# Nine-row partition pitch for the first two load groups of an RMSNorm-and-repeat kernel

## The chip, the cores and the metric

The kernel runs on one core of a Trainium2 chip. The metric is the device time of one execution in microseconds (us), lower is better. A comparison gives a median over several executions; a profile is one execution, recorded with times of every instruction and every DMA packet.

## The reference

The input `x` is 8 x 512 x 2048 in float32, that is 4096 rows of 2048 numbers (8 KB a row, 33.55 MB in all); `gamma` has 2048 numbers. Each row is repeated twice, divided by its root mean square and multiplied by gamma. The output has 8192 rows, 67.11 MB.

```python
x_rep = np.repeat(x, 2, axis=1)
rms = np.sqrt((x_rep ** 2).mean(axis=-1, keepdims=True) + 1e-6)
return (x_rep / rms * gamma[None, None, :]).astype(np.float32)
```

## The kernel before

The 4096 rows are handled in four groups of 1024 rows, n = 0 to 3. In a group each of the 128 SBUF partitions holds eight neighbouring rows of HBM: `load(n, at)` (L49) moves them with one DMA, 64 KB for a partition and 8.39 MB in all. A group is written in two halves, h = 0 and 1, of four rows a partition: `store(n, h, to)` (L52) writes the four rows twice over, again 64 KB a partition and 8.39 MB. So the program has four loads and eight stores of x's data, twelve DMAs of one size, and all of them are issued by SyncE's queue (SP) in the order of the code.

One SBUF tile `y` of 24 rows a partition is all the room there is. Its three regions of eight rows are called `first` (0 to 7), `second` (8 to 15) and `third` (16 to 23). The order of the work is written out by hand in `four(n, constants, step)` (L89), which does two groups and is called twice, with n = 0 and n = 2:

- Group n is loaded into rows 4 to 11, group n + 1 into `third`. The constants are made between the two issues.
- `squares` (L57) sums the squares of a row on ScalarE (ACT, L63) and takes the root (L67). `scale` (L70) takes the reciprocal on VectorE (DVE, L73) and multiplies a row by it and by gamma (L75), into every second row of a region. `repeat` (L80) copies each finished row to its neighbour (L82), on ACT or on DVE.
- The first half of group n goes to `first` and is stored from there, the second half to `second`. Then the first half of group n + 1 goes to `first`, the second to `third`.

Since all regions are reused, a load waits for the stores that still read its rows: the load of group 2 (rows 4 to 11) waits until the first half of group 1 has left `first`, the load of group 3 until the second half of group 1 has left `third`.

In the second region's repeat, `step` says whether DVE copies its two rows with one instruction (n = 0) or with two (n = 2).

`constants()` (L121) issues gamma's DMAs from ACT's queue: one of 16 pieces of 500 B, and three of 64 B each, into partition 0 of the rows 0 to 2 of `y`. Two GpSimd (POOL) partition broadcasts, L132 and L136, spread them from there to all partitions of `gamma_b`.

Of the kernel before, what the change touches and what calls it, by code (L numbers as in the profile page):

```python
# [1 line left out]

# [4 lines left out]


@with_exitstack
def kernel(  # L10
    ctx: ExitStack,
    tc: tile.TileContext,
    x: bass.AP,
    gamma: bass.AP,
    out: bass.AP,
):
    nc = tc.nc
    P = nc.NUM_PARTITIONS
    f32 = mybir.dt.float32
    Act = mybir.ActivationFunctionType  # L20
    Alu = mybir.AluOpType

    B, S, D = x.shape
    Bo, So, Do = out.shape
    R = So // S
    assert R == 2 and D == Do and B == Bo and So == S * R
    eps = 1e-6
    inv_d = 1.0 / float(D)


    K = 4
    N = B * S
    ntiles = N // (P * K)
    assert N % (P * K) == 0 and ntiles == 8
    H = 2
    x_t = x.rearrange("b s d -> (b s) d").rearrange("(n p k) d -> n p k d", p=P, k=H * K)
    out_t = out.rearrange("b s d -> (b s) d").rearrange("(n p h j) d -> n h p (j d)", p=P, h=H, j=K * R)

    singles = ctx.enter_context(tc.tile_pool(name="singles", bufs=1))
    rows = ctx.enter_context(tc.tile_pool(name="rows", bufs=1))  # L40
    junk = ctx.enter_context(tc.tile_pool(name="junk", bufs=1, space=bass.MemoryType.PSUM))
    small = ctx.enter_context(tc.tile_pool(name="small", bufs=4))

    y = rows.tile([P, 3 * K * R, D], f32, name="y")
    first, second, third = 0, K * R, 2 * K * R

    def load(n, at):  # L49
        nc.sync.dma_start(out=y[:, at : at + H * K, :], in_=x_t[n])  # L50

    def store(n, h, to):  # L52
        nc.sync.dma_start(
            out=out_t[n, h], in_=y[:, to : to + K * R, :].rearrange("p j d -> p (j d)")
        )

    def squares(at, rows):  # L57

        n = len(rows)
        ss = small.tile([P, n], f32, name=f"ss{n}")  # L60
        for c, k in enumerate(rows):
            sq = junk.tile([P, D], f32, name="sq")
            nc.scalar.activation(  # L63
                out=sq[:], in_=y[:, at + k, :], func=Act.Square, accum_out=ss[:, c : c + 1]
            )
        rms = small.tile([P, n], f32, name=f"rms{n}")
        nc.scalar.activation(out=rms[:], in_=ss[:], func=Act.Sqrt, scale=inv_d, bias=eps_t[:])  # L67
        return rms

    def scale(at, to, rows, rms):  # L70
        n = len(rows)
        rstd = small.tile([P, n], f32, name=f"rstd{n}")
        nc.vector.reciprocal(out=rstd[:], in_=rms[:])  # L73
        for c, k in enumerate(rows):
            nc.vector.scalar_tensor_tensor(  # L75
                out=y[:, to + R * k, :], in0=y[:, at + k, :], scalar=rstd[:, c : c + 1],
                in1=gamma_b[:], op0=Alu.mult, op1=Alu.mult,
            )

    def repeat(to, k0, k1, copy):  # L80
        y_r = y[:, to + R * k0 : to + R * k1, :].rearrange("p (k r) d -> p k r d", r=R)
        copy(out=y_r[:, :, 1, :], in_=y_r[:, :, 0, :])  # L82

    ctx.enter_context(tc.manual_schedule())

    half = K // 2
    up, down = list(range(K)), list(range(K - 1, -1, -1))

    def four(n, constants, step):  # L89


        load(n, first + K)
        constants()
        load(n + 1, third)
        for rows in (up[:half], up[half:]):
            scale(first + K, first, rows, squares(first + K, rows))
        repeat(first, 0, half, nc.scalar.copy)
        repeat(first, half, K, nc.vector.tensor_copy)
        store(n, 0, first)
        scale(second, second, down, squares(second, down))  # L100
        repeat(second, half, K, nc.scalar.copy)
        for k in range(0, half, step):
            repeat(second, k, k + step, nc.vector.tensor_copy)
        store(n, 1, second)
        roots = [squares(third + h * K, up) for h in range(H)]
        scale(third, first, up, roots[0])
        repeat(first, 0, half, nc.scalar.copy)
        repeat(first, half, K, nc.scalar.copy)
        store(n + 1, 0, first)
        scale(third + K, third, up, roots[1])  # L110
        repeat(third, 0, K, nc.scalar.copy)
        store(n + 1, 1, third)

    gamma_b = singles.tile([P, D], f32, name="gamma_b")
    G, E = 16, 3
    C = D // G - E
    gamma_s = y[0:1, 0:2, :].rearrange("p k (c d) -> p (k c) d", c=G // 2)
    gamma_t = y[0:1, 2, :]
    eps_t = singles.tile([P, 1], f32, name="eps_t")

    def constants():  # L121
        nc.scalar.dma_start(
            out=gamma_s[0:1, :, :C],
            in_=gamma[: G * C].rearrange("(p c d) -> p c d", p=1, c=G),
        )
        for c in range(E):
            at = G * C + c * G
            nc.scalar.dma_start(
                out=gamma_t[0:1, c * G : (c + 1) * G],
                in_=gamma[at : at + G].partition_broadcast(1),  # L130
            )
        nc.gpsimd.partition_broadcast(  # L132
            out_ap=gamma_b[:, : G * C].rearrange("p (c d) -> p c d", c=G),
            in_ap=gamma_s[0:1, :, :C],
        )
        nc.gpsimd.partition_broadcast(out_ap=gamma_b[:, G * C :], in_ap=gamma_t[0:1, : E * G])  # L136
        nc.vector.memset(eps_t, eps)  # L137

        root = singles.tile([P, 1], f32, name="root")[:]
        nc.scalar.activation(out=root, in_=eps_t[:], func=Act.Sqrt)  # L140

    four(0, constants, half)
    four(2, lambda: None, 1)


# [1 line left out]
_INS = ['x', 'gamma']  # L147
_OUTS = [((8, 1024, 2048), 'float32')]


# [23 lines left out]
```

## Time and profile before

| | us |
|---|---|
| median of 3 executions | 238.38 (238.24 to 238.87) |
| profiled execution | 238.07 |
| its span, first to last instruction or transfer | 236.2 |
| ACT busy | 110.2 (47%) |
| DVE busy | 84.5 (36%) |
| GpSimd busy | 2.8 (1%) |
| share of the 16 DMA engines' span taken by SP's packets (q1) | 98.7% |

The span lies 1.87 us under the profiled execution's own time, which in turn lies 0.31 us under the median. The table says how long each engine had something to do. Neither compute engine is at work for even half of the time; the DMA engines nearly always are.

### The profile page before, as it was taken

The page shows a single profiled execution, that of the slowest core. Times are in us where ns is not written, and L with a number is a line of the kernel's source. Part 1 is how long each engine was busy: PE and PEld are TensorE (multiplying, and loading weights), DVE is VectorE, ACT ScalarE, POOL GpSimd, SP SyncE. Part 2 cuts the span into 40 slices and gives each one's busy share as a digit, 9 for nine tenths or more (in the row PEclk, how much of TensorE's full clock was granted, in tenths as well). Part 3 has the DMA queues.
Part 4 walks back from the last instruction along what each step waited for, and adds up shares of the span by engine and source line. Part 5 has one row for each costly group of instructions (what it writes and reads, how often), then busy time and mean ns, then how long its engine had stood idle before and what let it go on. Part 6 is the DMA issues. An engine that isn't in the chain of part 4 may idle for free.

```text
span 236.2 us, 226 instructions
## 1 busy us (share of the span) xinstructions
DVE 84.5 (36%) x48; ACT 110.2 (47%) x86; POOL 2.8 (1%) x6
## 2 busy tenths in 40 slices
DVE  0000396594699500000000007928919992000000
ACT  2001989479998470000000049991999957400000
POOL 0110000000000000000000000000000000000000
DMA  9898989989898989989898998989898998989894
GB/s 355 356 533 355 510 377 422 466 366 522 355 533 356 533 355 422 466 377 510 355 533 355 488 400 355 533 355 533 355 533 355 488 399 355 533 355 533 355 533 178
DMA packets 1767, 100.68 MB, mean 426 GB/s; under 512 B 230, under 2 KB 230, under 8 KB 230
## 3 DMA queue, kind: packets, MB, share of 16 engines
q1 hardware_dynamic: 1728, 100.66, 98.7%
q10 hardware_dynamic: 38, 0.01, 0.0%
q14 instruction: 1, 0.01, 0.0%
HBM read 33.56 MB, written 67.11 MB: 426 GB/s over the span
## 4 chain that ended last, share of the span: by engine, by line
DMA 45%; ACT 26%; DVE 12%; issue 2%; DVEq 0%
DMA y<-in_x_dram 26%; DMA out_dram<-y 20%; ACT sq L63 15%; DVE y L75 12%; ACT y L82 11%; ACT rms L67 1%; DVE rstd L73 0%; DVEq L75 0%
## 5 line engine op out<-in xcount | busy, mean ns | idle before, releaser
L63 ACT ACTIVATE sq<-y 128x2048 f32<-128x2048 f32 x32 | 60.1, 1878 | 71.1 <-DMA y<-in_x_dram 70.4
L75 DVE SCALAR_TENSOR_TENSOR y<-y,rstd,gamma_b 128x2048 f32<-128x2048 f32 x32 | 73.8, 2349 | 1.6 <-DMA out_dram<-y 1.0
L82 ACT COPY y<-y 128x4096 f32<-128x4096 f32 (+1 forms) x10 | 42.6, 4283 | 19.1 <-DVE y L75 18.3
L73 DVE RECIPROCAL rstd<-rms 128x4 f32<-128x4 f32 (+1 forms) x10 | 1.7, 170 | 109.2 <-ACT rms L67 109.2
L82 DVE COPY y<-y 128x4096 f32<-128x4096 f32 (+1 forms) x5 | 9.2, 1865 | 0.1
L63 ACT ACTIVATION_READ_ACCUMULATOR sq<-y 128x1 f32 x32 | 6.0, 186 | 0.0
L67 ACT ACTIVATE rms<-ss,eps_t 128x4 f32<-128x4 f32 (+1 forms) x10 | 3.0, 297 | 0.3
L140 ACT ACT_TABLE_LOAD x1 | 1.3, 1283 | 2.6 <-issue 2.6
L132 POOL PARTITION_BROADCAST gamma_b<-y x1 | 2.2, 2243 | 10.2 <-DMA y<-in_gamma_dram 10.2
L136 POOL PARTITION_BROADCAST gamma_b<-y x1 | 0.3, 323 | 10.1 <-DMA y<-in_gamma_dram 10.1
L137 DVE MEMSET eps_t<- 128x1 f32 x1 | 0.1, 59 | 0.8 <-PEq L158 0.8
L140 ACT ACTIVATE root<-eps_t 128x1 f32<-128x1 f32 x1 | 0.2, 203 | 0.0
L158 POOL MEMSET const-bfloat16-1.0<- 128x1 bf16 x1 | 0.1, 102 | 0.0
L158 POOL MEMSET const-float32-0.0<- 128x1 f32 x1 | 0.1, 99 | 0.2 <-issue 0.2
L158 POOL MEMSET const-uint8-127<- 128x1 uint8 x1 | 0.1, 101 | 0.0
L158 POOL MEMSET const-float32-1.0<- 128x1 f32 x1 | 0.1, 98 | 0.0
## 6 DMA issues: line engine op xcount, KB each, us to landing
out_dram<-y SPq DMA_DIRECT2D x8, 24.8
y<-in_x_dram SPq DMA_DIRECT2D x4, 31.4
y<-in_gamma_dram ACTq DMA_DIRECT2D x3, 0.1 KB
y<-in_gamma_dram ACTq DMA_DIRECT2D x1, 7.8 KB, 9.8
```

Source lines behind the costliest of these rows:

```text
L63: nc.scalar.activation(out=sq[:], in_=y[:, at + k, :], func=Act.Square, accum_out=ss[:, c : c + 1])
L67: nc.scalar.activation(out=rms[:], in_=ss[:], func=Act.Sqrt, scale=inv_d, bias=eps_t[:])
L73: nc.vector.reciprocal(out=rstd[:], in_=rms[:])
L75: nc.vector.scalar_tensor_tensor(out=y[:, to + R * k, :], in0=y[:, at + k, :], scalar=rstd[:, c : c + 1], in1=gamma_b[:], op0=Alu.mult, op ...
L82: copy(out=y_r[:, :, 1, :], in_=y_r[:, :, 0, :])
L132: nc.gpsimd.partition_broadcast(out_ap=gamma_b[:, : G * C].rearrange("p (c d) -> p c d", c=G), in_ap=gamma_s[0:1, :, :C],)
L136: nc.gpsimd.partition_broadcast(out_ap=gamma_b[:, G * C :], in_ap=gamma_t[0:1, : E * G])
L137: nc.vector.memset(eps_t, eps)
L140: nc.scalar.activation(out=root, in_=eps_t[:], func=Act.Sqrt)
L158: nc = _bacc.Bacc("TRN2", target_bir_lowering=False, num_devices=1)
```

## The change

The rows 0 to 2047, groups 0 and 1, are dealt out to the partitions in another way. In HBM they are cut in two blocks. In the first block, 1152 rows, each partition owns nine neighbouring rows (72 KB). In the second block, 896 rows, it owns seven (56 KB). The first load takes the first eight of the nine, 64 KB a partition as before, but with 72 KB from one partition's start to the next one's. The second load becomes two DMAs: the ninth row (8 KB a partition, 1.05 MB), then the seven rows of the second block (56 KB, 7.34 MB).

The stores go to the places in the output that belong to these rows. The first half of group 1 has one row of the first block and three of the second, so this store becomes two DMAs: 16 KB a partition (2.10 MB) and 48 KB (6.29 MB). The other stores stay one DMA each; those of groups 0 and 1 have a partition pitch of 144 KB or 112 KB in the output instead of 128 KB. SP issues 14 DMAs instead of 12. Groups 2 and 3 are as before.

Gamma comes with two DMAs of 16 pieces of 256 B, into partition 0 of `gamma_b` itself, and one POOL broadcast spreads it from there. `step` is gone: DVE's copy of two rows of `second` is now two instructions in both calls of `four`.

```diff
-    x_t = x.rearrange("b s d -> (b s) d").rearrange("(n p k) d -> n p k d", p=P, k=H * K)
-    out_t = out.rearrange("b s d -> (b s) d").rearrange("(n p h j) d -> n h p (j d)", p=P, h=H, j=K * R)
+    x_r = x.rearrange("b s d -> (b s) d")
+    out_r = out.rearrange("b s d -> (b s) d")
+    C, T = H * K + 1, H * K - 1
+
+    def own(n):
+        if n == 0:
+            return [(0, C, 0, H * K)]
+        if n == 1:
+            return [(0, C, H * K, 1), (P * C, T, 0, T)]
+        return [(n * P * H * K, H * K, 0, H * K)]
+
+    def runs(view, n, k0, k1, r):
+        at, got = 0, []
+        for base, pitch, head, count in own(n):
+            a, b = max(k0, at), min(k1, at + count)
+            if a < b:
+                block = view[base * r : (base + P * pitch) * r].rearrange("(p k) d -> p k d", p=P)
+                got.append((a, b, block[:, (head + a - at) * r : (head + b - at) * r, :]))
+            at += count
+        return got
...
     def load(n, at):
-        nc.sync.dma_start(out=y[:, at : at + H * K, :], in_=x_t[n])
+        for a, b, rows in runs(x_r, n, 0, H * K, 1):
+            nc.sync.dma_start(out=y[:, at + a : at + b, :], in_=rows)
 
     def store(n, h, to):
-        nc.sync.dma_start(
-            out=out_t[n, h], in_=y[:, to : to + K * R, :].rearrange("p j d -> p (j d)")
-        )
+        for a, b, rows in runs(out_r, n, h * K, (h + 1) * K, R):
+            a, b = a - h * K, b - h * K
+            nc.sync.dma_start(
+                out=rows.rearrange("p j d -> p (j d)"),
+                in_=y[:, to + a * R : to + b * R, :].rearrange("p j d -> p (j d)"),
+            )
...
-        for k in range(0, half, step):
-            repeat(second, k, k + step, nc.vector.tensor_copy)
+        for k in range(half):
+            repeat(second, k, k + 1, nc.vector.tensor_copy)
...
     def constants():
-        nc.scalar.dma_start(
-            out=gamma_s[0:1, :, :C],
-            in_=gamma[: G * C].rearrange("(p c d) -> p c d", p=1, c=G),
-        )
-        for c in range(E):
-            at = G * C + c * G
-            nc.scalar.dma_start(
-                out=gamma_t[0:1, c * G : (c + 1) * G],
-                in_=gamma[at : at + G].partition_broadcast(1),
-            )
-        nc.gpsimd.partition_broadcast(
-            out_ap=gamma_b[:, : G * C].rearrange("p (c d) -> p c d", c=G),
-            in_ap=gamma_s[0:1, :, :C],
-        )
-        nc.gpsimd.partition_broadcast(out_ap=gamma_b[:, G * C :], in_ap=gamma_t[0:1, : E * G])
+        G, E = 16, 2
+        w = D // G // E
+        g_in = gamma.rearrange("(p c d) -> p c d", p=1, c=G)
+        g_to = gamma_b[0:1, :].rearrange("p (c d) -> p c d", c=G)
+        for c in range(0, D // G, w):
+            nc.scalar.dma_start(out=g_to[:, :, c : c + w], in_=g_in[:, :, c : c + w])
+        nc.gpsimd.partition_broadcast(out_ap=gamma_b[:], in_ap=gamma_b[0:1, :])
```

## The prediction

> **What bounds the kernel now.** I read the first page's span, DMA rows and queues first, because both compute engines are under 50%.
>
> ```profile
> span 236.2 us, 226 instructions
> DMA  9898989989898989989898998989898998989894
> q1 hardware_dynamic: 1728, 100.66, 98.7%
> q10 hardware_dynamic: 38, 0.01, 0.0%
> DMA 45%; ACT 26%; DVE 12%; issue 2%; DVEq 0%
> ```
>
> q1 is SP's queue: twelve DMAs of 8.39 MB (100.66 / 12). 1728 / 12 = 144 packets each: 128 of data, one for each partition (8.39 MB / 128 = 65,536 B), and 16 completion writes, one for each of the 16 DMA engines. They keep the engines busy for 98.7% of the span. The fifth line, the chain that ended last, gives 38% to ACT and DVE, which misleads: the chain follows who released whom, and does not say that the transfers stood still meanwhile. That is seen in stretches of one DMA's length. Columns: stretch, its length, busy us of DVE, ACT and POOL, clock, busy share of the DMA engines, GB/s.
>
> ```profile
> 1.70:21.60 19.90, 0.00 (x0) 1.49 (x2) 2.24 (x1) 1.00 1.01 422
> 21.60:40.95 19.35, 11.85 (x7) 17.35 (x16) 0.32 (x1) 1.00 1.00 434
> 40.95:60.30 19.35, 11.70 (x6) 14.29 (x14) 0.00 (x0) 1.00 1.00 434
> ...
> 79.65:99.00 19.35, 0.36 (x1) 7.02 (x1) 0.00 (x0) 1.00 1.00 434
> 99.00:118.35 19.35, 0.00 (x0) 0.00 (x0) 0.00 (x0) 1.00 1.00 430
> 118.35:137.70 19.35, 0.00 (x0) 0.00 (x0) 0.00 (x0) 1.00 1.00 434
> ...
> 215.10:234.45 19.35, 0.00 (x0) 0.00 (x0) 0.00 (x0) 1.00 1.00 434
> 234.45:236.23 1.78, 0.00 (x0) 0.00 (x0) 0.00 (x0) 1.00 0.01 0
> ```
>
> Each stretch is one of the twelve DMAs, in SP's order: load 0, load 1, store (0,0), and so on. Share 1.00 in every one, loads and stores alike, at 434 GB/s: the kernel is bytes over a fixed rate, 12 x 19.35 = 232.2 us. What is left of the span is small: 1.70 before the first byte, 0.55 more for the first load (19.90 against 19.35), about 1.8 at the end, and nothing between DMAs. The change moves the same 100.66 MB. So it can only change the cost of a packet, let the rings run dry, or touch these small remainders.
>
> **Cost of a packet.** Three very short stretches hold the start of just one packet each: of gamma's 500 B, of gamma's 64 B, and of 64 KB of x.
>
> ```profile
> 7.43:7.44 0.01, 0.00 (x0) 0.00 (x0) 0.00 (x0) 1.00 0.17 50
> 12.38:12.39 0.01, 0.00 (x0) 0.00 (x0) 0.01 (x1) 1.00 0.07 6
> 12.09:12.11 0.02, 0.00 (x0) 0.00 (x0) 0.02 (x1) 1.00 7.56 3277
> ```
>
> Share x 16 engines x length is the packet's time: 0.17 x 16 x 10 ns = 27 ns for 500 B, 0.07 x 16 x 10 = 11 ns for 64 B, 7.56 x 16 x 20 = 2419 ns for 65,536 B. From the first and the last, 36.8 ns are paid for 1000 B, and 27 - 18.4 = 8.6 ns for a packet of any size. From above, the 38 packets of q10 show 0.0% of 16 x 236.2 us, that is under 0.05% or 1.9 us: under 50 ns a packet.
>
> **Part by part.** Splitting load 1 adds 128 data packets, eight on each engine, and a completion write; splitting store (1,0) the same. 18 more on each engine x 8.6 ns = 0.15 us, on the path, since the engines have no slack. The ends are below: at 50 ns it is 0.9 us. I take 8.6 because 8 KB, 16 KB, 48 KB and 56 KB lie inside the sizes that the line goes through.
>
> Gamma goes from 38 packets to 2 x (16 + 16) = 64; 26 / 16 = 1.6 an engine, 0.01 us. For the rest it is hidden: the first POOL broadcast began at 10.65, the second at 23.01 for 0.32, and the first multiply, which needs both, at 27.34. After it, two DMAs must land instead of four behind the same 64 KB packets, so the one broadcast (2.24 + 0.32 = 2.6 us) should be over by 18 to 23 us, at least 4 us ahead of that multiply. Were that cover gone, each us past 27.3 would go to the store below. ACT issues two DMAs fewer and idles until 22.67 anyhow.
>
> The two single copies on DVE for the one double copy cost 2.36 - 2.29 = 0.07 us (the rows of the second and the first call). They release store (0,1), issued at 55.89, while store (0,0) occupies the engines until 60.3. Hidden by 4.4 us, less about 1.0 from an issue to its first byte (0.72 to 1.70).
>
> SP's queue gets two more issues of about 0.34 us. The one in load 1 is issued at about 1.5 us for data that move after 21.6. Of store (1,0), the small DMA waits for the first ACT copy (over at 72.6), the large one for the second, as now (issued at 76.17); they move after 79.65, and behind them store (1,1), issued at 87.08, is not needed before 99. Load 2 must now wait for two landings instead of one, at 100.04, with the engines taken by store (1,1) until 118.35. All of that is covered by more than 2 us.
>
> The one narrow place is store (0,0):
>
> ```profile
> 22.67 1.88 ACT L63 ACTIVATE sq<-y 128x2048 f32<-128x2048 f32 x1 [18.58 <-DMA y<-in_x_dram]
> 36.83 2.29 DVE L82 COPY y<-y 128x4096 f32<-128x4096 f32 x1
> 39.20 0.35 SPq L53 DMA_DIRECT2D out_dram<-y  x1
> ```
>
> Load 0 lands, 14.2 us of compute and the last copy follow, and SP issues at 39.20; with 1.0 us to the first byte, 40.2. The engines come free at 40.95. Slack 0.75 us. This compute is untouched, and the split makes load 1 slightly longer, so the slack grows by about 0.08. No cost.
>
> Pitch: before, the loads read at a 64 KB pitch and stores wrote at 128 KB, both at 434. The nearest rows for 72, 112 and 144 KB are these, so nothing; the ends are a gain of what load 0 loses (0.55) and the 430 stretch (19.35 x 4 / 434 = 0.18), together 0.73, and a loss as in the rivals.
>
> Sum: 238.07 + 0.15 + 0.01 = 238.2 for the profiled execution. The median was 0.31 above that execution, so 238.55.
>
> **Two rules of the Trainium skill**, which the sum does not use. "DMA: Bandwidth & Descriptors", section "Anatomy of one DMA", gives about 2.0 us of fixed cost for a DMA on GpSimd's path, and its "Rules for kernel authors" want few large transfers; unhidden, two more DMAs would by an estimate from that page add 4.0 us, 242.4. The trace's boundaries at 21.60, 40.95 and 60.30 show share 1.00 on both sides, so here I let the rows decide. [...]
>
> **The rivals.**
>
> Slower, by small packets. The 8 KB reads are the first run of short packets that the engines get in a row; before, short ones stood alone between 64 KB ones. If the time to reach HBM is hidden only by long packets, each of the 16 added packets of an engine pays some of it. The only row of such a time is load 0's 0.55 us: all of it on each is 16 x 0.55 = 8.8, 247; with 50 ns, 0.9 and 239.3. It decides from 0.72 / 16 = 45 ns a packet. Against it: the 27 ns for 500 B. Chance 0.17, centre 239.6.
>
> Slower, by a dry ring. If the new pitch slows load 0 so that it lands 0.75 us later or more while load 1 keeps its speed, store (0,0) comes too late, and every us beyond goes to the end on top of the load's own. Chance 0.04, from 239.2 up.
>
> Faster, by the pitch. Load 0's 0.55 and the 430 stretch go away: 238.55 - 0.55 = 238.0, with both 237.8. Since 1.0 us before the first byte and the rate stay, there is no more to be had. Chance 0.14, less than half of it (0.06) past 0.3%.
>
> Else my sum holds: 0.65.
>
> **How the numbers follow.** 0.3% (0.72 us) is about what a measurement of this kernel can tell from no change. Faster by more: 0.06, and 0.02 for a scatter of the medians, 0.08. Slower by more: 0.17 + 0.04 = 0.21. Within: 0.71. The likeliest case alone reaches 238.2 to 238.9, by the scatter of the three executions. The range takes in the pitch's gain to 237.8 below, and above the small packets' price at 50 ns with the scatter, to 239.6; some 0.06 lies under it and 0.12 over.
>
> **What would show it.** After: q1 with 14 x 144 = 2016 packets and the same MB; share 1.00 and 434 GB/s in all stretches but the first; about 427 to 433 in the 2.5 us of the ninth rows; store (0,0) issued near 39.2, its first byte without a gap; POOL done before 23 us; the span within 0.4 of 236.2. I am wrong if the stretch of the ninth rows takes over 3 us, if one with store (0,0) starts under share 1.00, or if the first load's 422 rises to 434.

## The result, and the profile after

The changed kernel takes 239.74 us (median of 6, 239.52 to 240.03) where the kernel before takes 238.39 (median of 6): the ratio is 1.0055, with a 95% interval from 1.0042 to 1.0068. It is slower by 1.35 us. I had forecast 238.55 and a range to 239.6. The profiled execution after took 239.88 us, 1.81 more than the one before; its span grew by as much, from 236.2 to 238.0.

First the page of the changed kernel: span, DMA row, and the queues q1 (SP: x's data) and q10 (ACT: gamma), with packets, MB and the share of 16 engines' span.

```profile
span 238.0 us, 223 instructions
DMA  9897999999898999999999898989898999999894
q1 hardware_dynamic: 2016, 100.66, 98.5%
q10 hardware_dynamic: 64, 0.01, 0.0%
```

2016 packets and 64 are as forecast, and so are the bytes. But 98.5% of 238.0 is 234.4 us of packet time, and 98.7% of 236.2 was 233.1: of the 1.8 us by which the span grew, the engines are busy for a little over 1 us longer with the same bytes, and stand still for the rest. Now the stretches of the changed kernel, again cut at the borders between the big DMAs (load 0, load 1 in its two parts, store (0,0), store (0,1), store (1,0) in its two parts, store (1,1), load 2, load 3, and so on).

```profile
1.70:21.50 19.80, 0.00 (x0) 1.49 (x2) 2.29 (x1) 1.00 1.02 424
21.50:40.90 19.40, 11.85 (x7) 16.67 (x16) 0.00 (x0) 1.00 1.00 432
40.90:60.50 19.60, 11.77 (x7) 14.55 (x13) 0.00 (x0) 1.00 0.99 428
...
79.88:99.34 19.46, 0.76 (x1) 7.02 (x1) 0.00 (x0) 1.00 1.00 431
99.34:119.24 19.90, 0.00 (x0) 0.00 (x0) 0.00 (x0) 1.00 1.01 422
119.24:139.05 19.81, 0.00 (x0) 0.00 (x0) 0.00 (x0) 1.00 0.99 423
139.05:158.37 19.32, 11.85 (x7) 16.99 (x16) 0.00 (x0) 1.00 1.00 435
...
216.33:235.65 19.32, 0.00 (x0) 0.00 (x0) 0.00 (x0) 1.00 1.00 434
```

The share says 1.00 nearly everywhere, as before, and would hide the loss; the last column shows it. Two stretches that ran at 430 and 434 now run at 422 and 423: store (1,1), whose place in the output changed, and load 2, whose place did not. From load 3 on all is as before.

The last engine to land is what the others wait for. It is read off what starts then: the first square of group 0 (load 0 landed), SP's issue of load 2 (store (1,0) landed) and of load 3 (store (1,1) landed), and the first square of group 2 (load 2 landed). Timeline, changed kernel:

```profile
23.35 1.88 ACT L85 ACTIVATE sq<-y 128x2048 f32<-128x2048 f32 x1 [19.86 <-DMA y<-in_x_dram]
100.66 0.34 SPq L69 DMA_DIRECT2D y<-in_x_dram  x1
120.53 0.34 SPq L69 DMA_DIRECT2D y<-in_x_dram  x1
140.57 1.88 ACT L85 ACTIVATE sq<-y 128x2048 f32<-128x2048 f32 x1 [52.87 <-DMA y<-in_x_dram]
```

In the kernel before the first of them was at 22.67; the other three:

```profile
100.04 0.34 SPq L50 DMA_DIRECT2D y<-in_x_dram  x1
119.74 0.34 SPq L50 DMA_DIRECT2D y<-in_x_dram  x1
138.85 1.88 ACT L63 ACTIVATE sq<-y 128x2048 f32<-128x2048 f32 x1 [51.79 <-DMA y<-in_x_dram]
```

Later by 0.68, 0.62, 0.79 and 1.72. So the loss comes in two parts: 0.68 us in load 0, kept for 80 us, and 1.1 more between the landing of store (1,0) and that of load 2. Then nothing is added (the span is longer by 1.8).

What happens in the second place is seen in the stretch that holds the start of the last 16 packets of store (1,1), one on each engine (GB/s x length is 1.05 MB, 16 x 64 KB). The share times the length is the mean duration of one packet. Before, then after:

```profile
115.80:116.60 0.80, 0.00 (x0) 0.00 (x0) 0.00 (x0) 1.00 3.23 1311
```

```profile
116.30:117.30 1.00, 0.00 (x0) 0.00 (x0) 0.00 (x0) 1.00 3.05 1049
```

3.23 x 0.80 = 2.58 us before and 3.05 after, where a 64 KB packet otherwise takes 2.42. Before, this last round was stretched by 0.17 us an engine; after, by 0.63. The first round of load 2, taken the same way from the packets, is stretched by 0.01 and by 0.19, and some engines start it late (before, then after):

```profile
118.69:119.10 0.41, 0.00 (x0) 0.00 (x0) 0.00 (x0) 1.00 5.93 2558
```

```profile
119.25:120.90 1.65, 0.00 (x0) 0.00 (x0) 0.00 (x0) 1.00 1.58 636
```

5.93 x 0.41 = 2.43 and 1.58 x 1.65 = 2.61 us.

### The profile page after: what moved, and what is told of

It is laid out like the page before. It is cut to its first block, busy times and chain, and to the rows that moved or that the text cites. A ratio compares the mean times of both kernels' runs of the same rounds, so it can differ in the third digit from the quotient of the medians.

```text
span 238.0 us, 223 instructions
## 1 busy us (share of the span) xinstructions
DVE 84.6 (36%) x49; ACT 110.2 (46%) x86; POOL 2.5 (1%) x5
## 3 DMA queue, kind: packets, MB, share of 16 engines
q1 hardware_dynamic: 2016, 100.66, 98.5%
## 4 chain that ended last, share of the span: by engine, by line
DMA 46%; ACT 24%; DVE 13%; issue 3%; DVEq 0%
DMA y<-in_x_dram 26%; DMA out_dram<-y 19%; ACT sq L85 15%; DVE y L97 13%; ACT y L104 9%; ACT rms L89 1%; DVE rstd L95 0%; DVEq L97 0%
## 5 line engine op out<-in xcount | busy, mean ns | idle before, releaser
L104 DVE COPY y<-y 128x2048 f32<-128x2048 f32 (+1 forms) x6 | 9.3, 1579 | 0.1
L146 POOL PARTITION_BROADCAST gamma_b<-gamma_b x1 | 2.3, 2294 | 15.8 <-DMA gamma_b<-in_gamma_dram 15.8
```

What stands on the lines that cost most here:

```text
L146: nc.gpsimd.partition_broadcast(out_ap=gamma_b[:], in_ap=gamma_b[0:1, :])
```

## The experiments

The theories go by letters in the expectations. A: the rows' new places in HBM, those of the writes or of the reads, disturb the transfers. B: the two gamma DMAs hold back the engines' start. C: the added DMAs and packets cost more than 8.6 ns each. D: engines that have drifted apart lose where reads follow writes. E: the pitch acts in another way than by that distance. F: a pitch that is no power of two does it. Ratios are against the kernel before in the same set of runs; there it had medians of 238.1 to 238.4.

**Which part of the change.**

e1_gamma_only is the kernel before with the new `constants()`:

```diff
+        for c in range(0, D // G, w):
+            nc.scalar.dma_start(out=g_to[:, :, c : c + w], in_=g_in[:, :, c : c + w])
+        nc.gpsimd.partition_broadcast(out_ap=gamma_b[:], in_ap=gamma_b[0:1, :])
```

> The kernel before with the change's gamma alone: two DMAs of 16 x 256 B into gamma_b, one broadcast. Theory A (row placement: the new places in HBM make writes and the read that follows them disturb each other) expects 238.4, no change. Theory B (start of the engines: the two gamma DMAs are dealt to all 16 engines while load 0 starts, and hold the last engine's first byte back, 2.92 us in the changed kernel against 2.24 before) expects the late first byte here too, load 0 landing near 23.3 instead of 22.7, and 0.4 to 0.6 more, 238.9. Theory C (the added packets and DMAs) expects 238.4.

238.94 us, ratio 1.0031 (1.0019 to 1.0043). No theory had that: load 0 landed early (first square at 22.57), so it is not B, yet 0.83 us are lost. Of these some 0.35 lie outside the span: time less span was 2.2 us in its executions, about 1.85 in those of the kernel before.

e2_rows_only is the changed kernel with the old `constants()`.

> The changed kernel with gamma as before (four DMAs, two broadcasts). A expects nearly the whole loss, 239.6, with the stretched last round of store (1,1) and first round of load 2. B expects that 0.4 to 0.6 of the loss is gone, 239.2, and load 0 landing near 22.7. C expects the whole loss, 239.7.

240.59 us, 1.0097 (1.0084 to 1.011); first square at 23.12, group 2's at 140.79. Both parts of the loss are there without the new gamma, so B falls. The rows cost more alone than with the gamma: the two parts of the change do not add up.

e4_reads_only has the changed kernel's loads, the old stores and the old gamma:

```diff
     def store(n, h, to):
-        for a, b, rows in runs(out_r, n, h * K, (h + 1) * K, R):
...
+        nc.sync.dma_start(
+            out=out_t[n, h], in_=y[:, to : to + K * R, :].rearrange("p j d -> p (j d)")
+        )
```

> Loads as in the changed kernel (nine-row pitch, load 1 in two DMAs), stores at the places of the kernel before in one DMA each, gamma as before; the output's first 2048 rows are thus in another order. A, if it is the writes' places: 238.4 to 238.5, stretch at the change from store (1,1) to load 2 as small as before (0.18 us an engine in sum). A, if it is the reads' places: 239.3. C: half of the packet cost, about 0.1, 238.5.

240.21 us, 1.0078 (1.0065 to 1.0091). e5_writes_only is the other half, the changed kernel's stores with the old loads and gamma:

```diff
     def load(n, at):
-        for a, b, rows in runs(x_r, n, 0, H * K, 1):
-            nc.sync.dma_start(out=y[:, at + a : at + b, :], in_=rows)
+        nc.sync.dma_start(out=y[:, at : at + H * K, :], in_=x_t[n])
```

> Loads as before, stores at the places of the changed kernel and store (1,0) in two DMAs, gamma as before; the output's first 2048 rows are thus in another order. A, if it is the writes' places: 239.2 to 239.4, with the last round of store (1,1) and the first of load 2 stretched by 0.7 to 0.9 us an engine in sum. C: 238.5 to 238.6.

238.52 us, 1.0015 (1.0007 to 1.0023). The reads make most of the loss of the rows, the writes a quarter of it at the most. I had leaned to the writes, because the place where the time goes is a store. With the reads alone store (1,1) writes where it always did, and still the last round is stretched (by 0.35 us an engine) and group 2's first square comes at 140.63.

e3_split_only splits load 1 and store (1,0) at their old places:

```diff
-        nc.sync.dma_start(out=y[:, at : at + H * K, :], in_=x_t[n])
+        for a, b in ((0, 1), (1, H * K)) if n == 1 else ((0, H * K),):
+            nc.sync.dma_start(out=y[:, at + a : at + b, :], in_=x_t[n][:, a:b, :])
```

and in the same way the store, at `R` of its `K * R` output rows.

> The kernel before, with load 1 in two DMAs (row 0 of a partition, then rows 1 to 7) and store (1,0) in two (one row, three rows), all at their old places. Theory C (added packets and DMAs) expects the loss here: the second issue behind load 0 and the smaller packets, 239.0 or more. Theory A (places) expects the price of the packets alone: 18 an engine x 8.6 ns = 0.15, so 238.3 beside 238.1 of the kernel before, load 0 landing by 22.7.

238.42 us, 1.0019 (1.0003 to 1.0036): 0.24 above the kernel before by the medians, for 0.15 expected. C, which expected 239.0 or more, falls by the medians. Yet three of the twelve executions took 239.57 to 239.98, where none of the kernel before passes 239.14 in this set: the split alone gives now and then a loss as large as the change's. e6_pitch_load0 leaves all DMAs whole and gives load 0 alone the pitch of nine rows:

```diff
+    x_9 = x.rearrange("b s d -> (b s) d")[: P * 9].rearrange("(p k) d -> p k d", p=P)
...
-        nc.sync.dma_start(out=y[:, at : at + H * K, :], in_=x_t[n])
+        rows = x_9[:, : H * K, :] if n == 0 else x_t[n]
+        nc.sync.dma_start(out=y[:, at : at + H * K, :], in_=rows)
```

> The kernel before, where load 0 alone takes the first eight of nine rows (pitch 72 KB); the other loads, one DMA each, stay, so some rows come twice and some never. Theory A, in the form that the reads of load 0 set it: the last engine finishes load 0 some 0.4 us later than before (23.0 to 23.3 landing instead of 22.65), the engines stay that far apart, the change from store (1,1) to load 2 is stretched by more than 0.3 us an engine in sum instead of 0.18, 239.0 to 240.0. Theory C expects 238.1, as before.

239.86 us, 1.0067 (1.005 to 1.0085), 1.68 us by the medians: a loss as large as the whole change's, from one load's addresses. The timeline shows the same two parts, 0.53 at load 0 and 2.26 by load 2:

```profile
23.20 1.88 ACT L65 ACTIVATE sq<-y 128x2048 f32<-128x2048 f32 x1 [19.12 <-DMA y<-in_x_dram]
141.11 1.88 ACT L65 ACTIVATE sq<-y 128x2048 f32<-128x2048 f32 x1 [53.65 <-DMA y<-in_x_dram]
```

and the last round of store (1,1) at 3.27 x 0.90 = 2.94 us a packet:

```profile
116.00:116.90 0.90, 0.00 (x0) 0.00 (x0) 0.00 (x0) 1.00 3.27 1165
```

**Which pitch, and where.** The same edit with other numbers of rows.

> The kernel before, where load 0 takes the first eight of sixteen rows (pitch 128 KB), so some rows come twice and some never. If any pitch that leaves gaps in HBM sets the engines apart, it costs as the 72 KB pitch did, 239.4 to 240.5. If it is the odd pitch, which no longer falls on a power of two, 238.2 as before.

Sixteen rows (`[: P * 16]`): 238.32 us, 0.9998 (0.9989 to 1.0007). No loss, though this load leaves gaps in HBM too.

> The kernel before, where load 0 takes the first eight of ten rows (pitch 80 KB); some rows come twice, some never. Theory F (a pitch that is no power of two lets the engines' streams run into each other) expects a loss as at 72 KB, 239.2 to 240.2. If only a pitch that is an odd number of rows does it, 238.3 as before.

Ten rows: 238.62 us, 1.003 (1.0013 to 1.0047), its twelve executions scattered from 238.22 to 240.09.

> The same with the first eight of twelve rows (pitch 96 KB). F expects a loss as at 72 KB, 239.2 to 240.2. If only pitches that are no multiple of 32 KB do it, 238.3.

Twelve rows: 238.79 us, 1.0033 (1.0016 to 1.005), from 238.13 to 240.42. Here the profile caught one of the long executions (239.79, first square 23.00, group 2's 140.47), and at ten rows one of the short (238.56; 22.75 and 138.84). So 80 and 96 KB give in some executions (four of twelve each above 239.2) the loss that 72 KB gave in all of its six, and in others none. By the medians they came out below what F expected, and not at "as before" either. Since e3_split_only had three such executions of twelve with the old pitch, these long ones cannot be put down to 80 and 96 KB for certain. F is not shown.

> The kernel before, where load 2 alone has the 72 KB pitch; some rows come twice, some never. If the pitch acts only where the kernel starts cold, 238.3 as before. If it acts wherever such a load begins, load 2 lands 0.3 us or more late and the stretch where it follows store (1,1) is over 0.5 us an engine in sum instead of 0.2, 238.8 to 239.8.

Load 2 alone at 72 KB: 238.38 us, 1.0007 (0.9997 to 1.0017). The 72 KB pitch costs nothing in load 2, which follows other transfers; it costs in load 0. Whether that lies in the cold start, in gamma's packets beside it or in these rows' place in HBM, no run separates.

e16_sixteen_rows deals both groups at sixteen rows a partition:

```diff
+        rows = x_16[:, n * H * K : (n + 1) * H * K, :] if n < 2 else x_t[n]
+        nc.sync.dma_start(out=y[:, at : at + H * K, :], in_=rows)
...
+        at = (n * H + h) * K * R
+        rows = out_16[:, at * D : (at + K * R) * D] if n < 2 else out_t[n, h]
```

> Groups 0 and 1 dealt with sixteen neighbouring rows to a partition: load 0 takes the first eight, load 1 the other eight, both at a pitch of 128 KB and one DMA each, the stores at 256 KB; gamma as before; the whole output is computed. F expects 238.3, as before (a load at 128 KB cost nothing, a store at 256 KB is new). If any new dealing of the groups costs something, 239 or more.

238.30 us, 1.0005 (0.9995 to 1.0014): a complete kernel with a new dealing of the rows and no loss by the medians. It is not faster than the kernel before either; nothing that I ran is.

**What load 0 leaves behind.** The table has every profile but those with a DMA, a wait or a copy added. In the last five, which have the whole loss, the first square starts at 23.0 or later, and group 2's at 140.4 or later:

| kernel | first square | group 2's | profiled us |
|---|---|---|---|
| sixteen rows, both groups | 22.50 | 139.61 | 239.01 |
| gamma only | 22.57 | 139.08 | 238.82 |
| sixteen rows, load 0 | 22.62 | 138.82 | 238.32 |
| split only | 22.62 | 139.15 | 238.52 |
| before | 22.67 | 138.85 | 238.07 |
| writes only | 22.68 | 138.88 | 238.35 |
| ten rows | 22.75 | 138.84 | 238.56 |
| nine rows, load 2 only | 22.92 | 138.93 | 238.15 |
| twelve rows | 23.00 | 140.47 | 239.79 |
| reads only | 23.10 | 140.63 | 240.23 |
| rows only | 23.12 | 140.79 | 240.26 |
| nine rows, load 0 only | 23.20 | 141.11 | 240.33 |
| after | 23.35 | 140.57 | 239.88 |

So a late last engine in load 0 goes with the second loss in full. Part of that loss comes without it: the profile of the kernel with sixteen rows in both groups caught one of its long executions, with the earliest first square of all, and yet its last round of store (1,1) is stretched by 0.34 us (3.07 x 0.90 = 2.76) and group 2 is 0.76 later than in the kernel before. To see whether a late engine makes the second loss, I made one engine late by hand: a DMA to one partition behind gamma, which is one packet on one engine.

Here `x_flat` is x as one list of 4096 rows.

```diff
+        nc.scalar.dma_start(
+            out=y[0:1, 12:16, :].rearrange("p k d -> p (k d)"),
+            in_=x_flat[0:4].rearrange("(p k) d -> p (k d)", p=1),
+        )
```

> The kernel before, plus one DMA of 32 KB into one partition's spare rows, behind gamma on ACT's queue: one packet, so one engine falls 1.21 us (half of 2.42) behind the others from about 25 us on. Theory D (engines that drift apart lose more where reads follow writes) expects the stretch at the change from store (1,1) to load 2 to grow from 0.18 to over 0.3 us an engine in sum, and the end to move by more than the 1.2 us itself, to 239.5 to 240. If distance does nothing by itself, the end moves by 1.2 at the most, less what that engine had in hand (the engines ended within 0.39): 238.9 to 239.3, stretch near 0.18.

240.47 us, 1.0092 (1.0078 to 1.0107): 2.3 us for a packet of 1.2. But the last round of store (1,1) was stretched by 0.19 us an engine (2.61 us a packet), little more than the 0.17 of the kernel before. The 1.1 us on top came at another place: the late engine's last packet of load 1 took 3.61 us instead of 2.42 (22.56 x 16 x 10 ns, in the stretch from 40.345 to 40.355). With 16 KB instead (`12:14`, `[0:2]`):

> The kernel before with 16 KB instead of 32 KB to one partition: one engine 0.61 us late, the distance that the nine-row kernels showed. Theory D expects losses like theirs at the change from store (1,1) to load 2, over 0.5 us an engine in sum, and 239.3 to 240. If a late engine alone does not do it, the end moves by 0.2 to 0.6, 238.4 to 238.8, and the stretch stays near 0.2.

239.45 us, 1.0045 (1.0033 to 1.0058), 1.0 us for a packet of 0.6, and a stretch of 0.17 at store (1,1), as before. In this profile a stretch of 10 ns holds the start of the late engine's last packet of load 1, when the others pass to store (0,0):

```profile
39.51:39.52 0.01, 0.00 (x0) 0.00 (x1) 0.00 (x0) 1.00 20.16 6554
```

20.16 x 16 x 10 ns = 3.23 us, 0.81 more than a packet takes. A lone late engine therefore paid twice at this place, where the others begin to write while it still reads; it did not bring about the loss at store (1,1). Nor is this a rule: at the next such place, from load 3 to store (2,0), the late engine's last read took 3.04 us with the 16 KB, but 2.42 with the 32 KB (from 157.46 on, the others writing from 158.3). D, in the form that any late engine does it, falls. The control has the same 32 KB as 16 packets:

```diff
+            out=y[0:16, 12, :512],
+            in_=x_flat[0:4].rearrange("k (c d) -> (k c) d", c=4),
```

> The same 32 KB as 16 packets of 2 KB, one on each engine: 0.075 + 0.01 + 0.01 us on each, none falls behind. All theories expect 238.2, within 0.2 of the kernel before.

238.83 us, 1.0029 (1.0018 to 1.004), more than I gave it (0.65 for 0.1). Its profiled execution (238.43) has load 0 landing 0.18 later and no engine far behind. So small edits ahead of load 0's landing move this kernel by some tenths, as the new gamma did.

Next I let the engines stand still after load 1 and start store (0,0) together:

```diff
+        if n == 0:
+            seen = small.tile([P, 1], f32, name="seen")
+            nc.vector.tensor_copy(out=seen[:], in_=y[:, third, 0:1])
         repeat(first, half, K, nc.vector.tensor_copy)
         store(n, 0, first)
```

> The kernel with the 72 KB pitch in load 0 alone, plus one tiny DVE copy that reads the second load's first column before the last copy ahead of store (0,0): this store is issued only when load 1 has landed on all engines, near 44.5, so the engines stand still for about 4 us and start it anew, together. Theory D (the pitch acts by the distance between engines that load 0 leaves) expects the stretch at the change from store (1,1) to load 2 back near 0.2 us an engine in sum, and the time within 0.3 of the next run, near 242.3. Theory E (the pitch acts in some other way, by places in HBM that stay open or by what is issued when) expects the stretch of 0.87 that the pitch alone gave, and 1.3 to 1.7 more than the next run, 243.8.

> The control: the kernel before with the same tiny copy. Both theories expect 238.1 + 4.2 = 242.3 (41.0 to 45.5 without transfers, less what overlaps), and a stretch of 0.2 at the change from store (1,1) to load 2.

243.85 us (1.0232, 1.0218 to 1.0246) with the pitch and 243.25 (1.0214, 1.0197 to 1.0231) without: 0.6 apart, where the pitch alone made 1.7. That store was issued at 44.98 and 44.35, also 0.6 apart, since load 1's last engine was still late by that much; so nearly all that is left is load 0's own lateness. E falls: after a common start the pitch has no second loss of its own. But D's stretch of 0.2 did not come either. With the pitch the last round of store (1,1) took 4.41 x 0.70 = 3.09 us a packet. The control surprised me more. Its last round:

```profile
120.25:121.00 0.75, 0.00 (x0) 0.00 (x0) 0.00 (x0) 1.00 4.11 1398
```

4.11 x 0.75 = 3.08 us a packet, a stretch of 0.66, as large as in the changed kernel. The engines had been set going within 0.25 us of each other (45.15 to 45.40). By this round they had drifted to starts within 0.60 us (120.30 to 120.90), about the 0.65 of the kernel before (115.85 to 116.50), which lost only 0.17. So how far apart the engines are does not settle the loss there; what about their standing does is not shown.

**What is lost at store (1,1).** Here reads from HBM first follow writes to HBM. In the last pair, load 2 is replaced by a copy inside SBUF of as many bytes:

```diff
+        if n == 2:
+            for half_at in (at, at + K):
+                nc.sync.dma_start(out=y[:, half_at : half_at + K, :], in_=y[:, second + K : second + 2 * K, :])
+            return
```

> The changed kernel, where load 2 is a copy of as many bytes inside SBUF (two DMAs of 32 KB a partition, finished rows of the second region into its place) and reads nothing from HBM; group 2 of the output is thus not computed from x. If reads from HBM that begin beside the last writes make the second part of the loss, the stretch of the last round of store (1,1) and of the first round after it is gone (under 0.1 us an engine in sum), and this kernel is only 0.3 to 0.8 above the next one. If the stretch belongs to the stores, it stays at 0.6 or more, and the distance at 1.3 or more.

> The kernel before with the same copy for load 2, as the control. If an SBUF copy runs at the rate of the other transfers (2.42 us for 64 KB), both theories expect 238.0 to 238.4; should it be slower, the distance to the run above is what counts.

250.85 us (1.053, 1.0515 to 1.0544) and 249.86 (1.0487, 1.0472 to 1.0501). The last round of store (1,1) in the changed kernel with the copy:

```profile
116.35:117.20 0.85, 0.00 (x0) 0.00 (x0) 0.00 (x0) 1.00 2.85 1234
```

2.85 x 0.85 = 2.42 us: no stretch at all, and in the kernel before the same (4.03 x 0.60 = 2.42). So the last writes are slow where reads from HBM come next, and not where a copy inside SBUF does. By the records they are slow before those reads start: in the kernel before, the first write of the round started at 115.86 and took 3.06 us, so that it was overdue from 118.28 on, and no packet of load 2 starts before 118.69. How the reads act ahead of their own packets, no run shows. The two times are 1.0 apart, between the 0.3 to 0.8 and the 1.3 that were expected; the copy runs at another rate and in another order on each engine, so this distance settles nothing.

## Why the prediction was wrong

Held in part: the dry ring. Store (0,0) was issued at 39.89, 0.69 later because load 0 landed 0.68 later. Its first byte followed after 1.2 us, not after the 1.0 that the slack of 0.75 was reckoned with, so the slack was 0.55. The first engines came free at 40.91; a stretch of the changed kernel from there on, in which x moves no byte yet, and its counterpart of the kernel before, where the next packets start at once:

```profile
40.91:41.08 0.17, 0.00 (x0) 0.17 (x1) 0.00 (x0) 1.00 0.01 0
```

```profile
41.00:41.17 0.17, 0.00 (x0) 0.17 (x1) 0.00 (x0) 1.00 1.78 771
```

So the leading engines stood still for 0.1 to 0.2 us, which is in the 428 GB/s of that stretch above. The last engines, which set the end, came free later and lost nothing by it. The rival's limit was 0.2 too high, and it was not what decided. One of the signs of being wrong that I had named did come: the stretch with store (0,0) has share 0.99.

Held: the cost of a packet. A stretch of the changed kernel with the start of one packet of 8 KB:

```profile
21.55:21.56 0.01, 0.00 (x0) 0.00 (x0) 0.00 (x0) 1.00 2.41 1024
```

2.41 x 16 x 8 ns (the stretch was 21.552 to 21.560) = 308 ns; the line through 500 B and 64 KB gives 36.8 x 8.19 + 8.6 = 310. The small-packet rival named the right sign and nearly the right time, 239.6, for a wrong reason, which is luck: short packets in a row pay nothing extra. Gamma's broadcast was done by 18.5, as expected.

Failed, and this decided: the step "Pitch". I put 72 KB at nothing because 64 and 128 KB both ran at 434 GB/s, and took these rows for near. By size they are; the runs show that in load 0 64 and 128 KB cost nothing and 72 KB alone costs 1.68 us (e6_pitch_load0). And I bounded what the pitch could do only by a gain of load 0's 0.55 and by the dry ring, so a load 0 that is late with no dry ring, 0.7 us on the path at once, had no case.

Failed: "nothing between DMAs". The share of 1.00 says that no engine stands still, not that packets take their 2.42 us. The one row that spoke, the stretch 99.00 to 118.35 at 430 GB/s, I counted as something that the change could only give back. It was a price that this kernel already paid, 0.17 us an engine at its one change from HBM writes to HBM reads, and it grew to 0.63, with 0.19 more in load 2's first round.

Failed as a size: gamma, which the sum has at 0.01 us. Alone it cost 0.83 (e1_gamma_only).

The Trainium skill ("DMA: Bandwidth & Descriptors", "Latency and other measured facts") has row pitches in HBM that are large powers of two as the ones that lose, from a little at 512 KiB to half the rate at 4 MiB, and a padding of 4 KiB as the cure. It gives no smaller pitch. In this kernel's first load it is the other way round: 64 and 128 KB lose nothing, and 64 KB padded by 8 KB gives the ratio 1.0067.

Open: why the first load at 72 KB lands 0.4 to 0.7 us late, and which order of the engines makes the change from writes to reads dear. The packet records do not name the engine. A late start of an engine is not by itself the reason: the last first packet of load 0 started after 2.90 in the changed kernel and before 2.26 in the kernel before, but also after 2.90 in the kernel with nine rows in load 2 only, which lost nothing. Also open is why the new gamma costs 1.0031 by itself, some of it outside the span, and yet the whole change costs less than its rows alone.

## What to carry to other kernels

In a kernel whose DMA engines are full, read GB/s beside the busy share, and compare when the last engine lands; a share of 1.00 covers packets that are stretched. Price a transfer only by rows with its own address pattern: a pitch between two that cost nothing may cost, and one load with the new pitch, everything else unchanged, tells it in one run, if that has executions enough: the split alone made three long ones among twelve. Where the first transfer of a kernel sets the engines apart, the bill may come much later, where reads and writes meet.

## What the runs showed of the hardware

The last 64 KB writes ahead of a load from HBM took 2.58 us in the kernel before and 3.05 after the change, but 2.42 when the load was a copy inside SBUF; so a change from HBM writes to HBM reads has a price. The writes pay it, and in the kernels that lost most the first reads too: 2.61 us in the changed kernel, 2.85 (2.59 x 1.10) in the one with the rows only. In the other direction a late engine's last read packet took 3.23 and 3.61 us while the others began to write, and 3.04 and 2.42 at the next such place.

A copy inside SBUF on the same queue was much slower than a transfer to or from HBM, 328 GB/s where those ran at 434 (the kernel before with the copy):

```profile
118.50:138.50 20.00, 0.49 (x2) 4.85 (x6) 0.00 (x0) 1.00 1.04 328
```
